# A decoder trunk on one core: the pooling mixer of layer 1 issued in another order, with three advances of the background work per pair of up products

## The chip, the cores and the metric

The kernel runs on one core of a Trainium2 chip. The metric is the device time of one execution, in microseconds, and less is better. The engines named below are TensorE (PE: matrix products), VectorE (DVE), ScalarE (ACT), GpSimd (POOL) and SyncE (SP: it issues the transfers).

## The reference

Sixteen meta tokens are put ahead of 1024 tokens of width 1024; two layers follow. Layer 0 mixes with multi-head latent attention, layer 1 with a causal pooling mixer. After each mixer comes a gated FFN, and RMSNorms stand before and after both.

```python
def pool_mixer(h, w_group, scale):          # windows 2, 4, 8, 16: one per group of 256 channels
    hf = h.reshape(B, L, 4, 256); csum = jnp.cumsum(hf, axis=1)
    means = [(csum_g - csum_g shifted by w) / min(t, w) for each group g, window w]
    mixed = stack(means) - hf
    return einsum('blgc,gcd->blgd', mixed, w_group).reshape(B, L, D) * scale
...
def conv_ffn(h, w_up, conv_w, conv_b, w_down):
    u = h @ w_up                             # 1024 -> 2 * 2816
    u = conv_b + sum(conv_w[j] * up[:, j:j + L] for j in range(3))     # causal
    gate, val = jnp.split(u, 2, axis=-1)
    return (jax.nn.silu(gate) * val) @ w_down
...
for i in range(2):
    m = mla_mixer(a, ...) if i == 0 else pool_mixer(a, ...)            # a = rmsnorm(h)
    h = h + rmsnorm(m);  f = conv_ffn(rmsnorm(h), ...);  h = h + rmsnorm(f)
```

## The kernel before

Channels lie on partitions and tokens along the free axis. The tokens go through in two halves, 536 and 504 of them. Every fp32 product is done as three products of a split into a high and a low part (`ah`, `al` for activations, `wh`, `wl` for weights): ACT casts the high part, DVE subtracts it to give the low part. A weight tile is loaded by SP, cast by ACT (`wh`) and finished by DVE (`wl`); `wh` and `wl` have four buffers each, the pooling weights `pwh` and `pwl` one each.

After attention the program is a row of dense stages: the output projection, then for each layer, each half and each of two parts an `ffn_up` (11 pairs of a gate and a value product, 8 weight blocks of three matmuls each, and each matmul in two cuts for half 0) and an `ffn_down`. An up product ends in PSUM; for half 0 it takes one of three tiles of two banks, for half 1 one of six tiles of one bank. ACT and DVE then apply the convolution (`cv`: one ACT row, two DVE rows), ACT the Silu, DVE the gate (`cv` times `cv`) and the low part `gl`. In layer 0, half 0, DVE first multiplies the product by the late norm factor (`u`).

All norms and the pooling mixer are generators in a list, `self.bg`. `tick()` advances the first of them by one step, that is to its next `yield`, and issues what the step holds with a priority 200 instructions ahead of the place in the code. Before the change `ffn_up` calls `tick()` twice per pair of products, `ffn_down` once per output block, and `drain()` runs what is left at the end of each stage. A scheduler then puts each engine's instructions into one order by these priorities. Each engine runs its own order strictly, so an instruction that waits holds all behind it on that engine.

A norm is `inv_rms_steps`: PE sums squares over channels into `ps_st`, DVE makes the reciprocal root (`nv`, `nyi`, `na`, `nb`, `ny`, `yh`, `yl`) and spreads it over two diagonal tiles (`diag`), PE multiplies these with ones (`ps_bc`), ACT copies the result to `R`. `post` multiplies the mixer's or FFN's output by `R` (`F`), adds it to the residual (`H`) and sums squares (`acc`). `poolmix` takes each of four groups of two channel blocks: `pa` is the normed block, one to four `psm` are window sums, `pmx` the mean less the block (for half 0 two short rows mend the first 16 tokens), and `xh`, `xl` its split. Then come two output blocks of the group's product (`xh`, `xl` with `pwh`, `pwl`). Half 0's mixer is advanced under the `ffn_up` of layer 0, half 1, part 0, and half 1's under that of layer 1, half 0, part 0; the second norm of layer 0's attention runs under that of layer 0, half 0, part 0.

Of the kernel before, what the change touches and what calls it, by code (L numbers as in the profile page):

```python
# [11 lines left out]
F32 = mybir.dt.float32  # L12
F32R = mybir.dt.float32r
I32 = mybir.dt.int32
ALU = mybir.AluOpType
# [6 lines left out]
KD = D // 128  # L22
# [24 lines left out]
class Kern:  # L47
# [561 lines left out]
    def dense(self):  # L609
        tc, nc, io, ctx = self.tc, self.nc, self.io, self.ctx  # L610
        P = lambda name, bufs, **kw: ctx.enter_context(tc.tile_pool(name=name, bufs=bufs, reuse_waits="tile", **kw))
        self.wp, self.ab, self.hp, self.gp = P("wp", 4), P("ab", 1), P("hp", 1), P("gp", 1)
        self.fp, self.up, self.tp = P("fp", 8), P("up", 2), P("tp", 5)
        stp = P("stf", 2, space=PSUM)
        self.stps = lambda name: stp.tile([128, 512], F32, tag="st", name=name)
        self.psum = None
        self.banks(1)
        self.dtile = lambda x: self.tp.tile([128, HALF], F32R, tag="x" + x, name="diag", bufs=2)
        self.H, self.A, self.bg = {}, {}, []

        F, acc = self.wo(0)
        self.bg.append(self.after_mixer(0, F, acc, 0, True))
        F, acc = self.wo(1)
        self.drain()
        self.bg.append(self.after_mixer(1, F, acc, 0, False))
        for L in range(2):
            self.L = L
            for hf in range(2):
                self.banks(2 - hf)
                Fa = None  # L630
                for part in range(2):
                    G = self.ffn_up(hf, part)
                    self.drain()
                    if part == 1 and hf == 0:
                        self.bg.append(self.pre(1, L))
                    if part == 1 and hf == 1 and L == 0:
                        self.bg.append(self.pre(0, 1))
                    if (L, hf, part) == (1, 1, 1):
                        self.ffn_down_last(part, G, Fa)
                        break  # L640
                    F, acc = self.ffn_down(part, G, Fa)
                    Fa = F
                    self.drain()
                else:
                    self.bg.append(self.after_ffn(hf, F, acc, L))
        self.drain()
# [13 lines left out]
    def after_mixer(self, hf, F, acc, L, pre):  # L660
        acc = yield from self.post(hf, F, acc, G_MIXPOST + 8 * L)
        if pre:

            self.late = yield from self.inv_rms_steps(acc, "xh", 2)
            yield from self.pre(hf, L, True)
        else:
            yield from self.ffn_norm(hf, acc)
# [14 lines left out]
    def inv_rms_steps(self, acc, tag, bufs=1, copy=True):  # L682
        yield
        st = self.inv_rms_a(acc, D)
        yield
        yield
        R = self.inv_rms_b(st, self.tp, tag, bufs, HALF, copy)
        yield
        return R[:, :acc.shape[1]]
# [138 lines left out]
    def post(self, hf, F, acc, gcol, last=False, c0=0, tag="Rp"):  # L828


        nc = self.nc
        R = yield from self.inv_rms_steps(acc, tag)
        acc = None
        for k in range(KD):
            nc.vector.scalar_tensor_tensor(F[k], F[k], self.par(gcol + k), R, op0=ALU.mult, op1=ALU.mult)
            h = self.H[hf][k]
            if last:
                s, n = (DEAD if hf == 0 else 0) + c0, F[k].shape[1]
                h = h[:, s:s + n]
            nc.vector.tensor_tensor(h, h, F[k], op=ALU.add)  # L840
            if last:
                s = (HALVES[1][0] - DEAD) * hf + c0
                nc.sync.dma_start(self.io["out"][:, k, s:s + n], h)
            else:
                acc = self.addsq(acc, h)
            if k % 2 == 1:
                yield
        return acc

# [39 lines left out]
    def ffn_up(self, hf, part):  # L889
# [8 lines left out]
        for jj in range(JH):  # L898
            j = part * JH + jj
            cv = []  # L900
            for gv in range(2):
                idx = gv * NJ + j
                u, = self.mm_half(self.wtile(io["w_up"][L, j, :, gv], KD), ah, al, skip=skip)
                if (L, hf) == (0, 0):
                    t = self.up.tile([128, HALF], F32, tag="u", name="u")
                    nc.vector.tensor_tensor(t, u, self.late, op=ALU.mult)
                    u = t
                p0 = G_CONV + (L * 2 * NJ + idx) * 4
                c = self.tp.tile([128, HALF], F32, tag="t", name="cv")[:, :n]
                nc.scalar.activation(c, u[:, pad:pad + n], AF.Identity, bias=self.par(p0 + 3), scale=self.par(p0 + 2))  # L910
                for x in (1, 0):

                    o = max(0, 2 - x - pad)
                    nc.vector.scalar_tensor_tensor(c[:, o:], u[:, pad + x - 2 + o:pad + x - 2 + n], self.par(p0 + x),  # L914
                                                   c[:, o:], op0=ALU.mult, op1=ALU.add)
                cv.append(c)
                if gv == 0:
                    nc.scalar.activation(c, c, AF.Silu)  # L918
                    self.tick()
            nc.vector.tensor_tensor(cv[0], cv[0], cv[1], op=ALU.mult)  # L920
            hi = self.gp.tile([128, HALF], F32R, tag=f"gh{jj}", name="gh")[:, :n]
            lo = self.gp.tile([128, HALF], F32R, tag=f"gl{jj}", name="gl")[:, :n]
            self.split(cv[0], hi, lo, lo_eng="dve")
            gh.append(hi)
            gl.append(lo)
            self.tick()
# [87 lines left out]
    def poolmix(self, hf, R):  # L1014
# [1 line left out]
        F, acc = [], None  # L1016
        n_tok = HALVES[hf][1]
        end = n_tok + 16
        for g in range(4):
            win = 2 << g  # L1020
            xh, xl = [], []
            for kk in range(2):
                k = 2 * g + kk
                a = self.tp.tile([128, HALF + 16], F32, tag="tc", name="pa")[:, :end]
                if hf == 0:
                    nc.gpsimd.memset(a[:, :16], 0.0)
                else:
                    nc.gpsimd.tensor_scalar(a[:, :16], self.phalo[:, k], 1.0, 0.0, op0=ALU.mult, op1=ALU.add)
                nc.vector.scalar_tensor_tensor(a[:, 16:], self.H[hf][k], self.par(G_MIXPRE + 8 + k), R,
                                               op0=ALU.mult, op1=ALU.mult)  # L1030
                if hf == 0:
                    nc.gpsimd.tensor_scalar(self.phalo[:, k], a[:, n_tok:end], 1.0, 0.0,
                                            op0=ALU.mult, op1=ALU.add)
                s = a
                for l in range(g + 1):
                    d = 1 << l
                    lo, hi = 2 * d - 1, end
                    n = self.tp.tile([128, HALF + 16], F32, tag="tc", name="psm")[:, :end]
                    nc.vector.tensor_tensor(n[:, lo:hi], s[:, lo:hi], s[:, lo - d:hi - d], op=ALU.add)
                    s = n  # L1040
                mx = self.tp.tile([128, HALF + 16], F32, tag="tc", name="pmx")[:, :end]
                nc.vector.scalar_tensor_tensor(mx[:, 16:], s[:, 16:], 1.0 / win, a[:, 16:],
                                               op0=ALU.mult, op1=ALU.subtract)
                if hf == 0:
                    nc.vector.tensor_tensor(mx[:, 16:32], s[:, 16:32], self.par(G_CNT + 16 * g, 16), op=ALU.mult)
                    nc.vector.tensor_tensor(mx[:, 16:32], mx[:, 16:32], a[:, 16:32], op=ALU.subtract)
                hi_ = self.tp.tile([128, HALF], F32R, tag="xh", name="xh", bufs=2)[:, :n_tok]
                lo_ = self.tp.tile([128, HALF], F32R, tag="xl", name="xl", bufs=2)[:, :n_tok]
                self.split(mx[:, 16:], hi_, lo_, lo_eng="dve")
                xh.append(hi_)  # L1050
                xl.append(lo_)
                if kk == 0:
                    W = self.wtile(io["w_pool"][g], 4, True)
                yield
            for m in range(2):
                ps = self.mm_half([W[2 * kk + m] for kk in range(2)], xh, xl)
                f = self.fp.tile([128, HALF], F32, tag="F", name="F")[:, :n_tok]
                self.evac(f, ps, self.par(G_PS + 2 * g + m))
                F.append(f)
                acc = self.addsq(acc, f)  # L1060
            yield
        return F, acc


# [50 lines left out]
```

## Time and profile before

| what | value |
|---|---|
| median of 3 runs | 2239.2 us (2238.68 to 2242.64) |
| the profiled execution's own time | 2242.48 us |
| span of its trace | 2240.7 us |
| PE busy in the span | 2151.0 us |
| DVE busy in the span | 1464.8 us |

The span is what the trace covers; 1.8 us of the profiled execution's time lie around it. The trace's times are those of one execution. Shares of busy time are means over stages with different limits.

### The profile page before, as it was taken

How to read it: one execution, taken by the hardware profiler on the slowest of the kernel's cores; microseconds unless marked ns; L12 is line 12 of the kernel's file. 1: busy time of each engine (PE TensorE's matmuls, PEld its weight loads, DVE VectorE, ACT ScalarE, POOL GpSimd, SP SyncE). 2: the span in 40 equal slices, each digit the busy share in tenths (PEclk: the TensorE clock that was granted, in tenths of full speed). 3: DMA queues.
4: the chain of work that ended last, by engine and by line, in shares of the span. 5: the costliest groups of instructions: out<-in, count | busy, mean ns of one | idle time of the engine just before them, and what ended most of it. 6: DMA issues, size and time to landing. Idle time of an engine off the chain costs nothing.

```text
span 2240.7 us, 36251 instructions
## 1 busy us (share of the span) xinstructions
PE 2151.0 (96%) x13890; PEld 1969.4 (88%) x13890; DVE 1464.8 (65%) x2711; ACT 1045.4 (47%) x1932; POOL 385.4 (17%) x732
## 2 busy tenths in 40 slices
PE   8889999998999999999998999999899999999996
PEld 8878888887989999999876888899899998888886
DVE  7877777776489726665877565587745557634656
ACT  6467777776464423433544344344434433433431
POOL 5567676764000000000000000000000000000001
PEclk9999999999999999999999999999999999999998
DMA  5011111114343232233222323422242245223231
GB/s 163 23 35 31 30 34 31 25 55 126 123 161 124 83 105 95 80 97 117 94 71 89 134 96 89 128 83 86 74 142 85 77 128 174 94 84 115 94 94 47
DMA packets 82901, 202.74 MB, mean 90 GB/s; under 512 B 10548, under 2 KB 31668, under 8 KB 82728
## 3 DMA queue, kind: packets, MB, share of 16 engines
q1 hardware_dynamic: 82584, 200.18, 28.4%
q8 instruction: 109, 1.79, 0.3%
q14 instruction: 64, 0.52, 0.1%
q10 hardware_dynamic: 144, 0.25, 0.0%
HBM read 179.15 MB, written 16.97 MB: 88 GB/s over the span
## 4 chain that ended last, share of the span: by engine, by line
PE 86%; DVE 5%; ACT 3%; DMA 2%; POOL 2%; issue 2%; DVEq 0%; SPq 0%; ACTq 0%; POOLq 0%
PE ps_m L766 71%; PE ps_t L587 2%; PE ps_s L536 2%; PE ps_o L572 1%; PE ps_s L538 1%; PE ps_o L573 1%; PE ps_s L537 1%; ACT P L550 1%; DVE ps_s L545 1%; DMA xt<-in_x 1%; PE ps_qk L417 1%; PE ps_qk L418 1%; PE ps_qk L419 1%; PE ps_st L84 1%; DMA or<-heads 0%
## 5 line engine op out<-in xcount | busy, mean ns | idle before, releaser
L70 DVE TENSOR_TENSOR wl<-wr,wh 128x1024 fp32r<-128x1024 f32 (+3 forms) x316 | 348.4, 1103 | 414.2 <-ACT wh L64 403.0
L64 ACT CAST wh<-wr 128x1024 fp32r<-128x1024 f32 (+3 forms) x316 | 301.1, 953 | 587.7 <-PE ps_m L766 513.9
L766 PE MATMUL ps_m<-ah,wh 128*128 128x506 f32 (+2 forms) x2112 | 564.7, 322 | 3.7 <-DVE cv L914 2.0
L766 PE MATMUL ps_m<-al,wh 128*128 128x506 f32 (+2 forms) x2112 | 567.4, 323 | 0.0
L766 PE MATMUL ps_m<-ah,wl 128*128 128x506 f32 (+2 forms) x2112 | 564.1, 321 | 0.0
L766 PEld LDWEIGHTS ps_m<-ah,wh 128*128 128x128 f32 x2112 | 354.2, 190 | 34.7 <-ACT cv L910 2.2
L766 PEld LDWEIGHTS ps_m<-al,wh 128*128 128x128 f32 x2112 | 354.0, 189 | 27.8
L766 PEld LDWEIGHTS ps_m<-ah,wl 128*128 128x128 f32 x2112 | 354.1, 189 | 27.5
L766 PE MATMUL ps_m<-gh,wh 128*128 128x268 f32 (+3 forms) x1088 | 289.1, 318 | 2.2 <-ACT F L775 2.2
L766 PE MATMUL ps_m<-gh,wl 128*128 128x268 f32 (+3 forms) x1088 | 288.0, 317 | 0.0
L766 PE MATMUL ps_m<-gl,wh 128*128 128x268 f32 (+3 forms) x1088 | 287.8, 317 | 0.0
L914 DVE SCALAR_TENSOR_TENSOR cv<-ps_m,params,cv 128x504 f32<-128x504 f32 (+1 forms) x264 | 196.1, 744 | 3.1
L766 PEld LDWEIGHTS ps_m<-gh,wh 128*128 128x128 f32 x1088 | 183.5, 190 | 15.8 <-ACT F L775 2.4
L766 PEld LDWEIGHTS ps_m<-gh,wl 128*128 128x128 f32 x1088 | 182.6, 189 | 13.7
L766 PEld LDWEIGHTS ps_m<-gl,wh 128*128 128x128 f32 x1088 | 182.9, 190 | 13.1
L64 ACT CAST gh<-cv 128x504 fp32r<-128x504 f32 (+2 forms) x88 | 54.7, 622 | 170.3 <-DVE cv L920 170.3
L550 ACT ACTIVATE P<-ps_s,stat 116x812 f32<-116x812 f32 (+9 forms) x160 | 111.4, 698 | 34.6 <-DVE stat L545 26.8
L587 PE MATMUL ps_t<-ident,P 116*116 116x116 f32 x720 | 114.5, 267 | 8.2 <-DVE ptl L601 4.7
L918 ACT ACTIVATE cv<-cv 128x504 f32<-128x504 f32 (+2 forms) x88 | 55.8, 635 | 139.3 <-DVE cv L914 139.3
L555 POOL TENSOR_SCALAR P<-P,stat 116x116 f32<-116x116 f32 (+2 forms) x144 | 108.0, 752 | 52.2 <-DVE stat L553 45.8
L869 POOL TENSOR_SCALAR al<-ahalo 128x2 fp32r<-128x2 f32 x16 | 5.4, 337 | 634.1 <-PE ps_m L766 634.0
L587 PEld LDWEIGHTS ps_t<-ident,P 116*116 116x116 f32 x720 | 83.6, 136 | 22.6 <-DVE ptl L601 5.4
(201 smaller groups left out, 3605.3 us busy)
## 6 DMA issues: line engine op xcount, KB each, us to landing
wr<-in_w_up SPq DMA_DIRECT2D x176, 512.0 KB, 3.5
wr<-in_w_down SPq DMA_DIRECT2D x56, 384.0 KB, 3.1
wr<-in_w_down SPq DMA_DIRECT2D x56, 320.0 KB, 2.9
wr<-in_w_o SPq DMA_DIRECT2D x16, 512.0 KB, 3.7
resid<-H SPq DMA_DIRECT2D x16, 268.0 KB, 4.1
H<-resid SPq DMA_DIRECT2D x16, 268.0 KB, 3.5
xt<-in_x SPq DMA_DIRECT2D x32, 130.0 KB, 2.3
resid<-H SPq DMA_DIRECT2D x16, 252.0 KB, 4.0
```

What stands on the lines that cost most here:

```text
L64: nc.scalar.copy(hi, src)
L70: eng.tensor_tensor(lo, src, hi.bitcast(F32), op=ALU.subtract)
L84: nc.tensor.matmul(ps[:w, i:i + 1], acc[:, w * i:w * i + w], self.ones, start=True, stop=True)
L417: nc.tensor.matmul(ps, wh, xh, start=i == 0, stop=False)
L418: nc.tensor.matmul(ps, wh, xl, start=False, stop=False)
L536: nc.tensor.matmul(ps[:n, x, :w], qh[:, qs], kh[:, ks], start=True, stop=False)
L550: nc.scalar.activation(dst, ps, AF.Exp, bias=mx[:n, 1:2], scale=-1.0, accum_out=es[:n, gi:gi + 1])
L555: nc.gpsimd.tensor_scalar(P[:n, :nk], P[:n, :nk], rs[:n], 1.0, op0=ALU.mult, op1=ALU.mult)
L587: nc.tensor.transpose(pt[:kn, x * QT:x * QT + n], Pi[:n, k0:k0 + kn], self.ident[:n, :n])
L766: nc.tensor.matmul(p, w, x[k][:, skip + c0:skip + c0 + m], start=k == 0 and w is wh and x is xh, stop=k == last and w is wl)
L914: nc.vector.scalar_tensor_tensor(c[:, o:], u[:, pad + x - 2 + o:pad + x - 2 + n], self.par(p0 + x), c[:, o:], op0=ALU.mult, op1=ALU.add)
L918: nc.scalar.activation(c, c, AF.Silu)
```

## The change

`ffn_up` calls its 8 weight blocks as two runs of 4, and on the value product a third `tick()` stands between the two. `post` yields after every fourth block instead of every second; `inv_rms_steps` has one more empty step between its two halves. `poolmix` is cut into `shape(g, kk)` (all that ends in `xh`, `xl`) and `products(g)`. The products of group g-1 are called in the step of the second block of group g, with their priority put 240 instructions back, where they stood behind their own group before, and the whole has nine steps instead of twelve. `xh`, `xl` and `diag` get three buffers instead of two; the pool of `u` is gone, and `u` shares the three buffers of `xl`.

```diff
@@ inv_rms_steps
         st = self.inv_rms_a(acc, D)
+        yield
         yield
         yield
@@ post
-            if k % 2 == 1:
+            if k % 4 == 3:
                 yield
@@ ffn_up
-                u, = self.mm_half(self.wtile(io["w_up"][L, j, :, gv], KD), ah, al, skip=skip)
+                W = self.wtile(io["w_up"][L, j, :, gv], KD)
+                ps = self.mm_half(W[:KD // 2], ah, al, 0, KD, skip=skip, n=n + pad)
+                if gv == 1:
+                    self.tick()
+                u, = self.mm_half(W[KD // 2:], ah, al, KD // 2, KD, ps, skip, n + pad)
                 if (L, hf) == (0, 0):
-                    t = self.up.tile([128, HALF], F32, tag="u", name="u")
+                    t = self.tp.tile([128, HALF], F32, tag="xl", name="u", bufs=3)
@@ poolmix
-        for g in range(4):
...
-            for m in range(2):
-                ps = self.mm_half([W[2 * kk + m] for kk in range(2)], xh, xl)
+        def products(g):
+            nonlocal acc
+            for m in range(2):
+                ps = self.mm_half([W[2 * x + m] for x in range(2)], *X[g])
...
+        for g in range(5):
+            for kk in range(2):
+                if g < 4:
+                    for dst, t in zip(X[g], shape(g, kk)):
+                        dst.append(t)
+                    yield
+                if g and kk == 0:
+                    self.ahead(-240, products, g - 1)
+                if g < 4 and kk == 0:
+                    W = self.wtile(io["w_pool"][g], 4, True)
+        yield
```

Three places show how the order moves. The number after a name counts tiles in the order in which they are made.

PE, layer 0, half 0, part 0, around the second norm of the attention's output, before (`ps_st` sums the squares, `ps_bc` spreads the factor; 72 rows of products stand between the two):

```order
L766 MATMUL ps_m_10230<-ah_9291,wh_10225 128x268 x2
L84 MATMUL ps_st_10056<-ones_66,acc_9697 126x1 x4
L766 MATMUL ps_m_10230<-al_9292,wh_10225 128x268 x2
...
L766 MATMUL ps_m_10420<-ah_9291,wh_10415 128x268 x2
L126 MATMUL ps_bc_10220<-diag_10216,ones_r_68 128x504
L766 MATMUL ps_m_10420<-al_9292,wh_10415 128x268 x2
```

The same place on PE in the changed program:

```order
L767 MATMUL ps_m_10099<-ah_9306,wh_10094 128x268 x2
L767 MATMUL ps_m_10099<-al_9307,wh_10094 128x268 x2
L767 MATMUL ps_m_10099<-ah_9306,wl_10095 128x268 x2
L84 MATMUL ps_st_9797<-ones_66,acc_9632 126x1 x4
L126 MATMUL ps_bc_9961<-diag_9957,ones_r_68 128x504
L126 MATMUL ps_bc_9961<-diag_9959,ones_r_68 128x504
L767 MATMUL ps_m_10161<-ah_9228,wh_10156 128x268 x2
```

And on DVE there (`wl_10351` is the weight tile of the fourth product after `ps_m_10099`, which takes the buffer that this one reads):

```order
L790 TENSOR_TENSOR acc_9632<-acc_9632,sq_9728 128x504
L70 TENSOR_TENSOR wl_10351<-wr_10349,wh_10350 128x1024
L86 TENSOR_SCALAR nv_9802<-ps_st_9797 126x4
L93 TENSOR_SCALAR nyi_9804<-nv_9802 126x4
...
L117 TENSOR_TENSOR diag_9957<-ident_61,yh_9952 126x504
L117 TENSOR_TENSOR diag_9959<-ident_61,yl_9953 126x504
L911 TENSOR_TENSOR u_10020<-ps_m_9971,R_9178 128x536
```

Between `ps_st` and `ps_bc` no product is left on PE, and DVE's order has a `wl` row ahead of `nv`.

PE, layer 0, half 1, part 0, the norm ahead of half 0's pooling in the changed program (`ps_m_14243` is the 11th up product of the part; before, 49 up matmuls stand between this `ps_st` and its `ps_bc`, and the first pooling product nearly two more up products behind that):

```order
L767 MATMUL ps_m_14243<-al_13312,wh_14238 128x506
L84 MATMUL ps_st_13987<-ones_66,acc_13874 67x1 x8
L767 MATMUL ps_m_14243<-ah_13311,wl_14239 128x506
L126 MATMUL ps_bc_14103<-diag_14099,ones_r_68 128x268
L126 MATMUL ps_bc_14107<-diag_14099,ones_r_68 128x268
L126 MATMUL ps_bc_14103<-diag_14101,ones_r_68 128x268
L126 MATMUL ps_bc_14107<-diag_14101,ones_r_68 128x268
L767 MATMUL ps_m_14273<-xh_14157,pwh_14181 128x268
L767 MATMUL ps_m_14274<-xh_14157,pwh_14181 128x268
```

The norm and the first pooling product now stand in one run, with one up matmul between.

PE, the same stage, the pooling products of one group before (up products, 128x506, stand between a group's first `xh` rows and its `xl` rows):

```order
L766 MATMUL ps_m<-ah,wl 128x506
L766 MATMUL ps_m<-xh,pwh 128x268 x4
L766 MATMUL ps_m<-ah,wh 128x506
...
L766 MATMUL ps_m<-ah,wl 128x506
L766 MATMUL ps_m<-xl,pwh 128x268 x2
L766 MATMUL ps_m<-xh,pwl 128x268 x2
L766 MATMUL ps_m<-xl,pwh 128x268 x2
L766 MATMUL ps_m<-xh,pwl 128x268 x2
L766 MATMUL ps_m<-ah,wh 128x506
```

The same in the changed program, from the end of the up product `ps_m_14518` to the start of the next one:

```order
L767 MATMUL ps_m<-ah,wl 128x506
L767 MATMUL ps_m<-xh,pwh 128x268 x4
L767 MATMUL ps_m<-xl,pwh 128x268 x2
L767 MATMUL ps_m<-xh,pwl 128x268 x2
L767 MATMUL ps_m<-xl,pwh 128x268 x2
L767 MATMUL ps_m<-xh,pwl 128x268 x2
L767 MATMUL ps_m<-xh,pwh 128x268 x4
...
L767 MATMUL ps_m<-xh,pwl 128x268 x2
L767 MATMUL ps_m<-xh,pwh 128x268 x4
L767 MATMUL ps_m<-ah,wh 128x506
```

And a piece of DVE's order that goes with it: these rows make the last block of group 1, the blocks of group 2 and the first of group 3 (of 26 rows between the second `cv` row of `ps_m_14518` and the last row of the block `pmx_14504`):

```order
L70 TENSOR_TENSOR xl_14368<-pmx_14363,xh_14367 128x536
L70 TENSOR_TENSOR wl_14803<-wr_14801,wh_14802 128x1024
L1044 TENSOR_TENSOR psm_14444<-psm_14442 128x549
L1044 TENSOR_TENSOR psm_14446<-psm_14444 128x545
L1047 SCALAR_TENSOR_TENSOR pmx_14448<-psm_14446,pa_14438 128x536
L1034 SCALAR_TENSOR_TENSOR pa_14492<-H_13704,params_70,R_14098 128x536
L1050 TENSOR_TENSOR pmx_14448<-psm_14446,params_70 128x16
L1044 TENSOR_TENSOR psm_14496<-pa_14492 128x551
L1051 TENSOR_TENSOR pmx_14448<-pmx_14448,pa_14438 128x16
```

Forty pooling matmuls (the second block of group 1, group 2, and the first four of group 3) stand on PE with no up matmul among them; before, every group's run was parted by up matmuls.

## Rows read from the trace of the kernel before

**Rows 1.** The page's first part: busy us, share of the span, instructions.

```profile
PE 2151.0 (96%) x13890; PEld 1969.4 (88%) x13890; DVE 1464.8 (65%) x2711; ACT 1045.4 (47%) x1932; POOL 385.4 (17%) x732
```

**Rows 2.** Waits of PE, 1102 to 1266 us: total us, times, longest.

```profile
PE ps_m L766 <- DVE psm L1039: 10.1, 1, 10.1
PE ps_m L766 <- ACT xh L64: 4.4, 2, 2.6
```

**Rows 3.** Waits of PE, 1447 to 1670 us.

```profile
PE ps_m L766 <- ACT xh L64: 2.7, 1, 2.7
PE ps_m L766 <- ACT F L775: 2.2, 1, 2.2
```

**Rows 4.** Windows: length, then busy us by engine; granted clock; DMA share, GB/s.

```profile
1102.80:1177.70 74.90, 70.48 (x322) 58.62 (x321) 59.36 (x99) 34.09 (x56) 2.24 (x12) 0.95 0.24 74
1177.70:1265.10 87.40, 77.28 (x375) 64.60 (x375) 56.61 (x108) 32.95 (x56) 0.92 (x3) 0.94 0.36 119
1265.10:1385.00 119.90, 119.90 (x526) 98.83 (x525) 72.64 (x90) 51.28 (x69) 0.00 (x0) 1.00 0.27 88
1584.80:1670.00 85.20, 80.08 (x616) 78.39 (x617) 48.06 (x87) 28.79 (x44) 0.00 (x0) 0.94 0.37 117
1189.80:1194.10 4.30, 4.21 (x13) 3.58 (x14) 3.44 (x8) 0.68 (x2) 0.00 (x0) 0.54 0.02 4
```

**Rows 5.** Timeline of PE: start us, us; in brackets the idle time before.

```profile
1146.65 1.26 PE L766 MATMUL ps_m<-xh,pwh 128*128 128x268 f32 x4 [2.62 <-ACT xh L64]
...
1152.76 0.43 PE L766 MATMUL ps_m<-ah,wh 128*128 128x506 f32 x1
...
1189.89 1.26 PE L766 MATMUL ps_m<-xh,pwh 128*128 128x268 f32 x4 [10.12 <-DVE psm L1039]
1190.95 0.62 PE L766 MATMUL ps_m<-gh,wh 128*128 128x504 f32 x1
...
1193.85 0.39 PE L766 MATMUL ps_m<-gl,wh 128*128 128x504 f32 x1
1194.08 0.39 PE L766 MATMUL ps_m<-gh,wl 128*128 128x504 f32 x1
```

**Rows 6.** Timeline of DVE: a run of `acc`, and a norm's chain.

```profile
643.67 4.53 DVE L789 TENSOR_TENSOR acc<-acc,sq 128x536 f32<-128x536 f32 x7
...
651.23 0.16 DVE L86 TENSOR_SCALAR nv<-ps_st 67x8 f32<-67x8 f32 x1
...
653.69 0.71 DVE L117 TENSOR_TENSOR diag<-ident,yh 67x536 fp32r<-67x536 f32 x1
654.32 0.71 DVE L117 TENSOR_TENSOR diag<-ident,yl 67x536 fp32r<-67x536 f32 x1
```

**Rows 7.** Timeline of PE at the kernel's end.

```profile
2227.21 0.81 PE L126 MATMUL ps_bc<-diag,ones_r 124*128 124x248 f32 x2 [3.20 <-DVE diag L117]
```

**Rows 8.** DVE by form, 1102.8 to 1177.7 us: busy us, mean ns of one.

```profile
L914 DVE SCALAR_TENSOR_TENSOR cv<-ps_m,params,cv 128x504 f32<-128x504 f32 x22 | 16.2, 734 | 0.1
L70 DVE TENSOR_TENSOR wl<-wr,wh 128x1024 fp32r<-128x1024 f32 x8 | 9.7, 1217 | 2.2 <-ACT wh L64 2.2
L1029 DVE SCALAR_TENSOR_TENSOR pa<-H,params,R 128x536 f32<-128x536 f32 x6 | 4.6, 770 | 0.3 <-ACT R L130 0.3
L1039 DVE TENSOR_TENSOR psm<-pa 128x551 f32<-128x551 f32 x6 | 4.4, 735 | 0.2
L1042 DVE SCALAR_TENSOR_TENSOR pmx<-psm,pa 128x536 f32<-128x536 f32 x6 | 4.2, 707 | 0.0
```

**Rows 9.** ACT by form, same stretch.

```profile
L910 ACT ACTIVATE cv<-ps_m,params 128x504 f32<-128x504 f32 x11 | 8.4, 767 | 0.0
L64 ACT CAST wh<-wr 128x1024 fp32r<-128x1024 f32 x8 | 8.4, 1053 | 14.2 <-PE ps_m L766 7.7 <-issue 6.5
L64 ACT CAST xh<-pmx 128x536 fp32r<-128x536 f32 x6 | 3.8, 630 | 0.0
```

**Rows 10.** Timeline of ACT: a norm's copy out of PSUM.

```profile
1112.75 0.67 ACT L130 COPY R<-ps_bc 128x268 f32<-128x268 f32 x2 [0.29 <-PE ps_bc L126]
```

More of the change, by code (lines that the diff above doesn't have):

```diff
@@ L612, in dense @@
         self.wp, self.ab, self.hp, self.gp = P("wp", 4), P("ab", 1), P("hp", 1), P("gp", 1)
-        self.fp, self.up, self.tp = P("fp", 8), P("up", 2), P("tp", 5)
+        self.fp, self.tp = P("fp", 8), P("tp", 5)
         stp = P("stf", 2, space=PSUM)
@@ L617, in dense @@
         self.banks(1)
-        self.dtile = lambda x: self.tp.tile([128, HALF], F32R, tag="x" + x, name="diag", bufs=2)
+        self.dtile = lambda x: self.tp.tile([128, HALF], F32R, tag="x" + x, name="diag", bufs=3)
         self.H, self.A, self.bg = {}, {}, []
@@ L662, in after_mixer @@
         if pre:
-            self.late = yield from self.inv_rms_steps(acc, "xh", 2)
+            self.late = yield from self.inv_rms_steps(acc, "xh", 3)
             yield from self.pre(hf, L, True)
@@ L1018, in poolmix, with shape @@
         end = n_tok + 16
-        for g in range(4):
+        def shape(g, kk):
             win = 2 << g
[L1021 to L1054, printed above, removed]
@@ new lines, in shape @@
+            k = 2 * g + kk
+            a = self.tp.tile([128, HALF + 16], F32, tag="tc", name="pa")[:, :end]
+            if hf == 0:
+                nc.gpsimd.memset(a[:, :16], 0.0)
+            else:
+                nc.gpsimd.tensor_scalar(a[:, :16], self.phalo[:, k], 1.0, 0.0, op0=ALU.mult, op1=ALU.add)
+            nc.vector.scalar_tensor_tensor(a[:, 16:], self.H[hf][k], self.par(G_MIXPRE + 8 + k), R,
+                                           op0=ALU.mult, op1=ALU.mult)
+            if hf == 0:
+                nc.gpsimd.tensor_scalar(self.phalo[:, k], a[:, n_tok:end], 1.0, 0.0,
+                                        op0=ALU.mult, op1=ALU.add)
@@ new lines, in shape @@
+            s = a
+            for l in range(g + 1):
+                d = 1 << l
+                lo, hi = 2 * d - 1, end
+                n = self.tp.tile([128, HALF + 16], F32, tag="tc", name="psm")[:, :end]
+                nc.vector.tensor_tensor(n[:, lo:hi], s[:, lo:hi], s[:, lo - d:hi - d], op=ALU.add)
+                s = n
+            mx = self.tp.tile([128, HALF + 16], F32, tag="tc", name="pmx")[:, :end]
+            nc.vector.scalar_tensor_tensor(mx[:, 16:], s[:, 16:], 1.0 / win, a[:, 16:],
+                                           op0=ALU.mult, op1=ALU.subtract)
@@ new lines, in shape @@
+            if hf == 0:
+                nc.vector.tensor_tensor(mx[:, 16:32], s[:, 16:32], self.par(G_CNT + 16 * g, 16), op=ALU.mult)
+                nc.vector.tensor_tensor(mx[:, 16:32], mx[:, 16:32], a[:, 16:32], op=ALU.subtract)
+            hi_ = self.tp.tile([128, HALF], F32R, tag="xh", name="xh", bufs=3)[:, :n_tok]
+            lo_ = self.tp.tile([128, HALF], F32R, tag="xl", name="xl", bufs=3)[:, :n_tok]
+            self.split(mx[:, 16:], hi_, lo_, lo_eng="dve")
+            return hi_, lo_
@@ L1060, in poolmix @@
                 acc = self.addsq(acc, f)
-            yield
+        X = [([], []) for _ in range(4)]
+        W = None
+        for g in range(5):
[9 more added lines that the diff above has]
+        yield
         return F, acc
```

## The prediction

> **What bounds the kernel now.** I read the page's first part, then the waits of PE, then the windows of the stages that the change touches, and last the timelines of PE and DVE at the single waits. PE is busy for 2151.0 of 2240.7 us [rows 1], so the time is PE's work plus the places where PE stands still or runs at the lower clock; the reader is to look for those places and not for busy engines. Outside the stretch from 1102 to 1670 us the change leaves the dense stages as they are, but for one norm in layer 0, half 0. In a stage with no mixer beside it PE never stops: 119.90 busy of 119.90, DVE busy for 72.64 of that [rows 4], and 526 matmuls in that time are 0.228 us each, or 5.47 for an up product of 24.
>
> Half 0's pooling costs PE 10.1 + 4.4 us of waiting in three waits [rows 2]. Behind two of them the matmuls stay slow for a while: from 1189.89 to 1193.85 us stand four pooling matmuls and seven of 504 columns, which at the 0.23 us between the two rows at 1193.85 and 1194.08, and 0.12 for the shorter ones, need 2.1 us, so 1.9 of the 4.0 are lost [rows 5]. The granted clock there is 0.54 [rows 4], near the lower of the two levels, 1.2 GHz. In the same way the 6.1 us from 1146.65 to 1152.76 (four short matmuls and twelve of 506) lose 2.9 [rows 5]. Sum of half 0: 14.5 + 4.8 = 19.3. Half 1's stretch from 1584.8 has PE busy for 80.08 of 85.20 at a mean clock of 0.94 [rows 4]: 5.1 of idle time, of which [rows 3] name 4.9, and up to as much again in slow matmuls, so about 10. So 29 us is all that a perfect pooling mixer could give back.
>
> **The change part by part.** Work is neither added nor removed: matmuls, DVE rows, casts, loads and stores are the same in number, and cutting an up product into two calls adds no matmul. The third buffers take no time. The transfers of pooling weights and residual blocks move by a few rows in SP's queue; no wait of PE in [rows 2, 3] is put down to a transfer, so I cost that at nothing; the cover is the weight buffers, and if it went, the next up product would be late. What counts is the order: three steps per pair bring the mixer to its end within one part, where a rest used to run in the drain behind it. In half 0, by the order's counts, 59 DVE rows come forward into the time of the last twelve up products. At start-to-start prices (a run of seven `acc` takes 4.53 us, 0.65 each though one lasts 0.71 [rows 6]; `wl` 1.14, `pa` 0.69, `psm`, `pmx` and `cv` 0.65, each its duration less that overlap [rows 8]; small rows of a norm 0.20, from twelve or so between 651.23 and 653.69 [rows 6]) they come to 29.8 us, on top of the 59.4 that DVE already works in 74.9 [rows 4]: 89 us of DVE against about 73 of PE. PE's order sets what that costs.
>
> Term A, the norm in layer 0, half 0. `ps_bc` now stands straight behind `ps_st`. DVE has the `wl` of the fourth product ahead in front of `nv`, and that takes the buffer which `ps_m_10099` has only just released. So behind `ps_st` come a cast of 1.05 [rows 9], a `wl` of 1.14, and the chain from `nv` to the end of the second `diag`, 651.23 to 655.03, 3.8 us [rows 6]: 6.0, with 0.1 for the start of the matmul 6.1. Slow matmuls behind it cost 1.9, the smaller of the two losses above, or 2.9. I take 8.0. The only place where the trace has `ps_bc` behind `ps_st` with nothing between is the kernel's end, where PE waits 3.20 [rows 7]; that is the lower bound (the `wl` already done, no loss of clock), and 9.0 the upper. What was hidden before by some 17 us of products is now bare.
>
> Term B, half 0's mixer. Behind the norm's `ps_st` one up matmul is left. DVE then has eight small rows of the chain (1.6), the two `cv` rows of `ps_m_14243` which wait for its end and for ACT's first row (0.77 + 0.65 + 0.65) and two `diag` (1.3): 5.0 us before `ps_bc` can start. The first pooling product follows directly: the copies to `R` (0.7 [rows 10]), `pa`, `psm`, `pmx`, the next block's `pa` and `psm` and two short rows (3.7 by [rows 8]), and the cast `xh` (0.63 [rows 9]), 5.1 us with PE doing only `ps_bc`. Then one up product and the rest of group 0 run, and group 1's first block beside two up products, with DVE ahead. After `ps_m_14518` come the forty pooling matmuls. Its second `cv` row ends 2.8 us behind it (a `cv` of ACT, two of DVE with a `pmx` between). From there to the block `pmx_14504` DVE has 26 rows, among them two `wl`, nine `psm`, three `acc` and three `xl`, 15.2 us; a cast makes it 18.6 until group 3's first matmul. PE's 36 matmuls ahead of that are 36 x 0.12 = 4.4. PE so waits 14.2 there, in four or five pieces. What is held behind them is the next up product, so also its `cv` and gate. Waits in sum 5.0 + 5.1 + 14.2 = 24.3; slow matmuls behind the two stretches at 2.4 each, the mean of 1.9 and 2.9: 4.8. Against 19.3 before: +9.8. Bounds: if DVE is far enough ahead that the 14.2 vanish, 10.1 + 2.4 - 19.3 = -7; if group 3's second block makes another wait as long as one of the pieces, +14.
>
> Term C, half 1's mixer. Its norms keep their products between `ps_st` and `ps_bc`, and each group's products are parted by up products. DVE's rows in the time of twelve up products come to 84.1 by the same prices, PE's to 80.2: 3.9 of waiting at least, with two slow stretches 8.7, against 10 before: -1.5, between -10 (all hidden) and +4.
>
> Sum 8.0 + 9.8 - 1.5 = +16.3. On the profiled execution that is 2242.5 + 16.3 = 2258.8; this execution is 3.3 over the median of the runs, 2239.2, so I forecast 2255. With all lower bounds 3.2 - 7 - 10 = -14, with all upper ones +27.
>
> **The rivals.** First, a gain. The products of a group now stand a step behind the shape of its last block, so `xh` and `xl` could be done when PE comes to them. The three waits of [rows 2] were all of that kind, and PE has six tiles to run on, so DVE may lag by several products of 5.47 us before an up product is held; an excess of 16 us of DVE would fit into that and be worked off under `ffn_down`, where DVE has 28 us less to do than before. Half 0's 19.3 would vanish and term A stay at its bare chain: 2239.2 - 19.3 + 3.2 = 2223. The Trainium skill speaks for this: its page "Perfetto Trace Analysis", section "Optimization Strategy", says that where the most-contended engine changes over time, interleaving such stretches may help. Here the mixer's stretch was already interleaved and DVE busy for 59.36 of 74.90 there [rows 4]. Against this rival stands the run of forty matmuls: PE is in order, so no tile helps while a pooling matmul waits at the head. It decides if DVE reaches `pmx_14504` within 4 us of the end of `ps_m_14518` instead of 18.
>
> Second, no change: the stalls only move. If DVE's excess of 16 us is the whole loss of half 0 in place of 19.3, term A is the bare 3.2 and half 1 stays, the sum is -0.1: 2239.
>
> Third, heavier: term A at 9, term B at +14 and half 1 at +4, as each norm and each group waits with a loss of clock behind it: 2266. For it speaks that two of three waits in [rows 5] and [rows 2] had such a loss; against it, that half 1's products are spread.
>
> **How the numbers follow.** The forecast, 2244 to 2262, has a chance of 0.54; the heavier case, 2262 and more, 0.10; no change, within 0.2% or 4.5 us (about what a measurement of this kernel can tell from nothing), 0.18; the gain 0.18. The range of 8 in 10 runs from 2229, which leaves out the better half of the gain, to 2267, above the sum of all upper bounds. Slower 0.64, same 0.18, faster 0.18. The likeliest case's own range is 2244 to 2262.
>
> **What the profile after would show.** Term A: a wait of PE at `ps_bc` for `diag` of 5 to 6.5 us under layer 0, half 0's `ffn_up`; 3 would say that the `wl` came early. Term B: a second such wait of about 5 ahead of half 0's pooling, a wait of about 5 for the first `xh`, and four or five waits for `xh`, `xl` of 2 to 4.5 between two up products, with a granted clock near 0.5 behind each stretch; a window of DVE there near full, and the drain behind with far less of DVE than before. Term C: small waits, none over 4. The prediction is wrong if the waits for `xh` and `xl` are gone (the gain), or if PE's wait for `diag` is absent in both places; a wait for a `cv` or `u` by an up product would be a cause that I did not count.

## The result, and the profile after

The changed kernel takes 2262.76 us (median of 4 runs, 2260.96 to 2264.61), the kernel before in the same sessions 2240.27. The ratio is 1.0097, with a 95% interval of 1.0085 to 1.011: slower by 22.5 us, on the side that was forecast and inside the range of 8 in 10 runs (2229 to 2267), but 0.8 us above the likeliest case's own range of 2244 to 2262, and 6 us more than the sum gave. The profiled execution has a span of 2260.7 us, 20.0 more than that of the kernel before, whose profiled execution lay 2.2 us above its median.

The page's first part, to be read beside [rows 1]:

```profile
PE 2156.9 (95%) x13890; PEld 1973.3 (87%) x13890; DVE 1465.0 (65%) x2711; ACT 1046.6 (46%) x1932; POOL 390.0 (17%) x732
```

The counts are the same, and DVE's busy time too (1465.0 to 1464.8): nothing was added. PE's busy time is 6 us longer with the same matmuls, since more of them ran at the lower clock; the rest of the 20 us of span is idle time. The waits of PE, from three stretches (layer 0, half 0; layer 0, half 1; layer 1, half 0), beside [rows 2, 3]:

```profile
PE ps_bc L126 <- DVE diag L117: 4.1, 1, 4.1
...
PE ps_m L767 <- ACT xh L64: 15.5, 4, 5.3
PE ps_bc L126 <- DVE diag L117: 4.4, 1, 4.4
PE ps_m L767 <- DVE xl L70: 1.8, 1, 1.8
...
PE ps_m L767 <- ACT xh L64: 4.8, 3, 2.9
PE ps_m L767 <- DVE xl L70: 2.6, 2, 1.4
PE ps_m L767 <- DVE cv L919: 2.6, 2, 1.4
PE ps_m L767 <- ACT F L778: 1.3, 2, 0.8
```

The first stretch had no wait at all before. In the second, 14.5 us of waits have become 21.7: two of them are the bare norm (4.4 for `diag`) and the longest `xh` (5.3) right behind it. In the third, 11.3 us stand where the two rows of [rows 3] name 4.9, and all waits of that stretch before 7.9. These rows of the kernel before belong to it: the window of the first stretch (columns as in [rows 4]), and the waits of the third that [rows 3] leave out.

```profile
643.00:741.00 98.00, 97.98 (x798) 97.81 (x799) 85.98 (x159) 44.63 (x61) 0.00 (x0) 1.00 0.38 126
...
PE ps_m L766 <- DVE cv L914: 2.0, 1, 2.0
PE ps_m L766 <- DVE xl L70: 0.7, 1, 0.7
PE ps_m L766 <- ACT F L777: 0.3, 1, 0.3
```

The windows of the changed kernel show what DVE did and what clock was granted:

```profile
714.50:720.90 6.40, 6.26 (x24) 5.55 (x25) 6.40 (x11) 3.41 (x5) 0.00 (x0) 0.50 0.23 71
...
1095.00:1143.00 48.00, 38.38 (x188) 32.26 (x186) 36.94 (x69) 18.56 (x29) 2.20 (x9) 0.86 0.13 41
1118.60:1123.60 5.00, 4.91 (x14) 4.11 (x15) 4.62 (x11) 0.91 (x3) 0.72 (x2) 0.50 0.00 0
1143.00:1163.00 20.00, 7.92 (x33) 6.76 (x32) 19.39 (x33) 10.61 (x20) 6.78 (x6) 0.61 0.34 114
1163.00:1178.00 15.00, 15.00 (x67) 12.71 (x66) 8.40 (x14) 5.29 (x10) 0.38 (x1) 0.83 0.17 56
...
1540.00:1570.00 30.00, 24.45 (x148) 22.37 (x147) 27.42 (x42) 13.84 (x22) 1.81 (x3) 0.83 0.28 92
```

From 1143 to 1163 us PE works for 7.92 of 20.00 us while DVE works for 19.39: the run of forty. PE's timeline names the pieces, with the bare norm of layer 0, half 0 ahead of it:

```profile
709.46 1.04 PE L84 MATMUL ps_st<-ones,acc 128*126 128x1 f32 x8
714.64 1.38 PE L126 MATMUL ps_bc<-diag,ones_r 126*128 126x504 f32 x2 [4.14 <-DVE diag L117]
...
1148.32 1.26 PE L767 MATMUL ps_m<-xh,pwh 128*128 128x268 f32 x4 [4.66 <-ACT xh L64]
1151.39 0.82 PE L767 MATMUL ps_m<-xl,pwh 128*128 128x268 f32 x2 [1.82 <-DVE xl L70]
1156.99 1.26 PE L767 MATMUL ps_m<-xh,pwh 128*128 128x268 f32 x4 [3.44 <-ACT xh L64]
1162.20 1.26 PE L767 MATMUL ps_m<-xh,pwh 128*128 128x268 f32 x4 [2.17 <-ACT xh L64]
```

These are the four pieces that the prediction spoke of, 12.1 us in sum. DVE at the bare norm:

```profile
710.32 1.23 DVE L70 TENSOR_TENSOR wl<-wr,wh 128x1024 fp32r<-128x1024 f32 x1 [0.91 <-ACT wh L64]
711.46 0.15 DVE L86 TENSOR_SCALAR nv<-ps_st 126x4 f32<-126x4 f32 x1
...
713.91 0.68 DVE L117 TENSOR_TENSOR diag<-ident,yh 126x504 fp32r<-126x504 f32 x1
714.50 0.68 DVE L117 TENSOR_TENSOR diag<-ident,yl 126x504 fp32r<-126x504 f32 x1
```

`ps_st` ends at 710.5, the `wl` ahead of `nv` at 711.5, and the chain at 715.2. Only 1 us of the `wl` is on the path, since the cast ran beside `ps_st`. The first `ps_bc` starts at 714.64, when the first of the two `diag` is done (714.59), and the second at 715.2, when the other is.

### The profile page after: what moved, and what is told of

Same layout as the page of the kernel before. It is cut to its first block, busy times and chain, and to the rows that moved or that the text cites. A ratio compares the mean times of both kernels' runs of the same rounds, so it can differ in the third digit from the quotient of the medians.

```text
span 2260.7 us, 36223 instructions
## 1 busy us (share of the span) xinstructions
PE 2156.9 (95%) x13890; PEld 1973.3 (87%) x13890; DVE 1465.0 (65%) x2711; ACT 1046.6 (46%) x1932; POOL 390.0 (17%) x732
## 4 chain that ended last, share of the span: by engine, by line
PE 83%; DVE 7%; ACT 3%; DMA 2%; issue 2%; POOL 2%; SPq 0%; DVEq 0%; ACTq 0%; POOLq 0%
PE ps_m L767 70%; PE ps_t L587 2%; PE ps_s L536 2%; PE ps_o L572 1%; PE ps_o L573 1%; PE ps_s L538 1%; PE ps_s L537 1%; ACT P L550 1%; DMA xt<-in_x 1%; DVE ps_s L545 1%; PE ps_qk L417 1%; PE ps_qk L418 1%; PE ps_qk L419 1%; DMA or<-heads 0%; PE ps_bc L126 0%
## 5 line engine op out<-in xcount | busy, mean ns | idle before, releaser
L70 DVE TENSOR_TENSOR wl<-wr,wh 128x1024 fp32r<-128x1024 f32 (+3 forms) x316 | 348.4, 1102 | 435.3 <-ACT wh L64 431.9
L915 ACT ACTIVATE cv<-ps_m,params 128x504 f32<-128x504 f32 (+1 forms) x132 | 101.5, 769 | 9.9 <-PE ps_m L767 9.9
```

The costliest lines, as they stand in the source:

```text
L70: eng.tensor_tensor(lo, src, hi.bitcast(F32), op=ALU.subtract)
```

## The experiments

Three theories stood against each other. **Theory 1**: the third advance per pair draws the halves of a norm together and brings the pooling products into long runs that wait for DVE. **Theory 2**: putting the products a step back makes the waits. **Theory 3**: the shared buffers of `u` and `xl` do. The kernel before took 2240.3 to 2241.5 in the sessions, as a median of 4 to 17 runs.

### The third advance taken out

```diff
-                if gv == 1:
-                    self.tick()
```

> The changed kernel with the third advance per pair taken out, all else kept. Theory 1 (the third advance draws the norms' two halves together and packs the pooling products into one run of forty): the order now has 7 and 11 us of products between the sums and the spread in the two norms, and no run over 24 matmuls, so the time is 2232 to 2244. Theory 2 (putting the products a step back makes the waits): no less than 2255. Theory 3 (the shared buffers of u and xl): 2263.

Measured: 2223.54 us (2223.24 to 2225.78), ratio to before 0.992 [0.9906, 0.9933]. It beats both kernels, by 17.9 us the one before and by 39.2 the changed one, which is more than theory 1 expected. Theories 2 and 3 fall as causes by themselves: all that they name is still there. Its waits of PE in the two mixer stretches:

```profile
PE ps_m L767 <- ACT xh L64: 5.5, 2, 3.2
PE ps_m L767 <- DVE xl L70: 0.9, 1, 0.9
...
PE ps_m L767 <- DVE cv L917: 4.1, 2, 2.1
PE ps_m L767 <- ACT F L778: 0.3, 1, 0.3
```

No `diag` is left there, and 6.4 us of product waits stand where there were 14.5 before.

### Three more empty steps in each norm

```diff
         yield
         yield
         yield
+        yield
+        yield
+        yield
         R = self.inv_rms_b(st, self.tp, tag, bufs, HALF, copy)
```

> The changed kernel with three more empty steps between the two halves of each norm. Both bare norms get products between their halves again (7 and 11 us by the order), the run of forty stays. Theory 1: the norm of layer 0, half 0 gives back its 7.6 us and the one ahead of half 0's pooling about 5, the forty keep their waits of some 18: 2247 to 2253. Theories 2 and 3: no change, 2263.

Measured: 2239.62 us (2237.58 to 2242.60), ratio 0.9992 [0.9984, 1.0001]. It gives back 23.1 us, about ten more than theory 1 expected, and against theories 2 and 3. I had not counted that the 5.3 us wait for the first `xh` is part of the bare norm (it is gone here; the three `xh` waits of the run of forty are still there, 4.7 the longest). So the two norms and what hangs on them cost most of 23 us, and the run of forty stays.

### The pooling mixer of before, with three advances

```diff
-            self.ahead(-240, products, g - 1)
+            for m in range(2):
+                ps = self.mm_half([W[2 * kk + m] for kk in range(2)], xh, xl)
```

> The changed kernel with the pooling mixer of before (products right behind their group's shapes, twelve steps), the third advance kept. Both norms stay bare in the order, and each group's products stand in a run of twenty with four ahead. Theory 1: the bare norms keep 7.6 and about 7 us and the four runs wait for their own group's rows, 2255 to 2270. Theory 2: 2240 to 2248, since the products are no longer put back. Theory 3: 2263.

Measured: 2272.33 us (2270.34 to 2274.92), ratio 1.0136 [1.0122, 1.015]. Slower by another 9.6: against theories 2 and 3, and 2 us over theory 1's range.

### The pooling mixer of the change alone

The kernel before with `poolmix` replaced, two buffers for `xh` and `xl`, and nothing else:

```diff
-            for m in range(2):
-                ps = self.mm_half([W[2 * kk + m] for kk in range(2)], xh, xl)
...
+                if g and kk == 0:
+                    self.ahead(-240, products, g - 1)
```

> The kernel before with the pooling mixer of the change alone (nine steps, products a step back), two advances per pair, all buffers and norms of before. Theory 1: no wait is added and the products' waits shrink, 2230 to 2242. Theory 2: 2250 or more. Theory 3: 2240.

Measured: 2227.72 us (2224.38 to 2230.22), ratio 0.9935 [0.9923, 0.9948]. It is 2 us below theory 1's range, and against theories 2 and 3: the mixer of the change is a gain of 14 us by itself. What in it gains is not shown by this run, since the products stand a step back and the mixer has nine steps instead of twelve. In the kernel before, the longest wait, the 10.1 us of [rows 2], stands behind the last up matmul of the part and ahead of the first of `ffn_down`, where the rest of the mixer is drained (24 pooling matmuls stand in one run there, so not every group was parted by up matmuls before); here all pooling products are through before the first of `ffn_down`, and that wait is gone. Nine steps alone may do that. The 4.2 us from here to the run with two advances lie in the buffers, `post`'s longer steps, the added step in the norm and the two calls per up product together; which of them it is was not tried.

### The third advance alone

The kernel before with the two runs of four blocks and the tick between, and nothing else:

```diff
+                ps = self.mm_half(W[:KD // 2], ah, al, 0, KD, skip=skip, n=n + pad)
+                if gv == 1:
+                    self.tick()
+                u, = self.mm_half(W[KD // 2:], ah, al, KD // 2, KD, ps, skip, n + pad)
```

> The kernel before with the third advance per pair alone (the value product in two runs of four blocks, an advance between); pooling mixer, norms and buffers of before. In the order the norm ahead of half 0's pooling is bare, the norm in layer 0, half 0 keeps its products, each pooling group is a run of twenty with four ahead. Theory 1: the time of the run with the old mixer, 2272, less its 7.2 us for the norm in layer 0: 2260 to 2268. Theory 2 (putting back is needed for a loss): 2241.

Measured: 2271.56 us (2269.79 to 2273.20), ratio 1.0135 [1.0122, 1.0148]. So +30.7 us on the kernel before, some 4 over the expected range; on the changed kernel it is +39.2. Most of the difference is the norm of layer 0, half 0, which is not bare here (6.1 us, by the runs with the third advance in one stage). The wait for `diag` ahead of the mixer is 6.9 here, and each of half 0's four groups waits for its own `xh`; the last three rows are DVE's wait in the stretch of the last three of these, the window of that stretch, and the window of the 7.45 us wait in it:

```profile
PE ps_m L766 <- ACT xh L64: 31.6, 7, 7.5
PE ps_bc L126 <- DVE diag L117: 6.9, 1, 6.9
...
DVE acc L789 <- ACT sq L788: 11.8, 2, 6.0
...
1126.50:1186.00 59.50, 39.56 (x174) 33.20 (x174) 42.73 (x72) 22.09 (x36) 1.87 (x9) 0.86 0.17 60
...
1146.90:1154.90 8.00, 0.55 (x3) 0.13 (x1) 8.00 (x15) 3.38 (x5) 0.32 (x2) 0.82 0.29 108
```

DVE is busy all through the wait, but only for 42.73 of the 59.50 us: in these it waits 11.8 us for the squares of the pooling products (`acc` for `sq`). With each group's products right behind its shapes, PE and DVE wait for each other in turn; a DVE that is full is not the whole cause here.

### The products not put back by 240

```diff
-                    self.ahead(-240, products, g - 1)
+                    self.ahead(0, products, g - 1)
```

> The changed kernel with the products' priority put back by nothing instead of 240, still a step behind their group. The order keeps both bare norms and a run of forty. Theory 1: within 4 us of the changed kernel, 2259 to 2267, since the run of forty comes from three advances per pair. Theory 2: 2240 to 2250.

Measured: 2264.84 us (2260.54 to 2267.55), ratio 1.0104 [1.009, 1.0117]: as the changed kernel, by theory 1.

### The products put back by 480, three more empty steps

```diff
-                    self.ahead(-240, products, g - 1)
+                    self.ahead(-480, products, g - 1)
```

> The changed kernel with three more empty steps in each norm and the products put back by 480 instead of 240. In the order a run of 28 and one of 44 now stand 11 us of up products later. Theory 1a (the run waits because it stands ahead of DVE's rows): the 18 us of waits and slow matmuls of the run shrink to under 4, and half 1's 13 to under 5, 2212 to 2225. Theory 1b (DVE has 16 us more work than PE in that stretch, wherever the products stand): the waits go over to the up products for their cv rows, 2232 to 2240.

Measured: 2238.36 us (2235.85 to 2241.60), ratio 0.9989 [0.9981, 0.9998]. That is the time of the run with three empty steps alone (2239.62). The traces show why: against that run, the 480 did not move the head of the run. In both, 432 up matmuls of the part stand ahead of it (336 in the changed kernel), and the long waits fall at the same times, first in the run with the three empty steps alone, then in this one:

```profile
1149.61 1.26 PE L770 MATMUL ps_m<-xh,pwh 128*128 128x268 f32 x4 [4.75 <-ACT xh L64]
1158.53 1.26 PE L770 MATMUL ps_m<-xh,pwh 128*128 128x268 f32 x4 [4.18 <-ACT xh L64]
```

```profile
1149.40 1.26 PE L770 MATMUL ps_m<-xh,pwh 128*128 128x268 f32 x4 [3.61 <-ACT xh L64]
1158.36 1.26 PE L770 MATMUL ps_m<-xh,pwh 128*128 128x268 f32 x4 [4.54 <-ACT xh L64]
```

The waits for `xh`, `xl` and `pwh` come to 12.4 us there and 11.8 here. So theory 1a was not put to the test: that products further behind DVE's rows would wait less is neither shown nor ruled out. By time it is 1b, but not by its place: the waits stay at `xh` and do not go over to the `cv`. The windows of this run:

```profile
1095.00:1145.00 50.00, 49.53 (x249) 41.75 (x248) 44.14 (x80) 23.40 (x37) 2.28 (x9) 1.00 0.20 65
1145.00:1163.00 18.00, 7.25 (x31) 6.09 (x29) 17.23 (x30) 9.54 (x19) 1.14 (x5) 0.62 0.30 100
```

DVE is busy for 44.1 of 50.0 us ahead of the run and for 17.2 of 18.0 in it, so it has little room to catch up.

### The products put back by 480, two advances

The third advance taken out as in the first experiment, and 480 as in the one above.

> Two advances per pair with the mixer of the change and its products put back by 480. Theory 1: the 10.3 us that the run with two advances and 240 still loses at three product waits from 1163 to 1178 shrink to under 3: 2213 to 2219. If DVE is the limit there: 2222 to 2225.

Measured: 2226.06 us (2222.95 to 2232.14), ratio 0.9934 [0.992, 0.9948]: no gain over 240, and 1 us above the range for DVE as the limit. One `xh` wait of 5.5 us is left. Its product stands behind 504 up matmuls of the part, as the same product does with 240, so this run does not decide between the two either.

### The third advance in one stage alone

Three kernels, each with two advances elsewhere; the pair in brackets is (0, 0), (0, 1) and (1, 0).

```diff
-                if gv == 1:
+                if gv == 1 and (L, hf) == (0, 0):
```

> The changed kernel with the third advance kept only in layer 0, half 0, two advances elsewhere. In the order only the norm there is bare. Theory 1: the run with two advances everywhere, 2223.5, plus the 7.6 us that the trace of the changed kernel loses there: 2229 to 2233. If the loss of that norm is hidden once the rest is spread: 2223.

> The third advance kept only in layer 0, half 1, where half 0's mixer runs: bare norm ahead of the mixer and the run of forty. Theory 1: the trace loses 31.7 us in that stage with three advances and 10.3 with two, so 2223.5 + 21.4 = 2245, from 2241 to 2249.

> The third advance kept only in layer 1, half 0, where half 1's mixer runs. Theory 1: 17.1 us of loss there with three advances, 6.2 with two, so 2223.5 + 10.9 = 2234, from 2230 to 2238. The forecast had this stage at no loss, which would be 2222 to 2225.

Measured: 2229.68 us (2227.70 to 2232.68), 2244.93 (2243.04 to 2250.51) and 2232.95 (2231.68 to 2236.85), with ratios to before of 0.9949 [0.9936, 0.9961], 1.002 [1.0012, 1.0029] and 0.9965 [0.9951, 0.9978]. Over the 2223.54 of two advances that is 6.1, 21.4 and 9.4 us, all in their ranges; the sum, 36.9, is 94% of the 39.2 that the third advance costs in all three places. The one wait for `diag` in the first of them is that of the changed kernel:

```profile
PE ps_bc L126 <- DVE diag L117: 4.2, 1, 4.2
```

### Two advances, products not put back by 240

The third advance taken out, and 0 in place of 240.

> Two advances per pair, mixer of the change, products a step behind their group but with their priority put back by nothing. If the step behind is what helps: 2220 to 2227. If the 240 instructions are needed on top: 2230 to 2240, as the products then wait for their rows as in the kernel before.

Measured: 2226.72 us (2225.42 to 2227.56), ratio 0.9934 [0.9921, 0.9946]. It is in the range for the step behind; the 240 add some 3 us. That it is the step behind, and not the nine steps, stays argued: both are kept here.

## Why the prediction was right, and where it was off

**The direction and its cause** held: the order brings work of DVE forward into a stretch where DVE has little room, and PE, in order, waits at the norm and at the run of forty. The forecast sum was +16.3, measured +22.5. A tally over the traces (for each matmul, how much later than is usual for its form the next one starts) gives for the three stages, each with the `ffn_down` behind it, 1.9, 20.3 and 14.7 us before and 9.4, 31.9 and 17.5 after: +7.5, +11.6 and +2.8, for the terms +8.0, +9.8 and -1.5. The sum, 21.9, is more than the 20.0 us of span, since what lies ahead of these stages took 1.9 less in this execution.

**Term A** (8.0) was right in place and near in size: 6.1 by the run that has the third advance only there. Its two parts were off in opposite ways, so its size is in part luck. The wait was 4.1 and not 6.1, because the cast of the `wl` ran beside `ps_st` and the first `ps_bc` did not wait for the second `diag`; the slow matmuls cost about 3.1, not 1.9 (24 matmuls in 6.26 us at a granted clock of 0.50).

**Term B** (29.1 of loss after, +9.8) held piece by piece: 4.4 for 5.0, 5.3 for 5.1, 12.1 in four waits for 14.2. What was too small is the clock. I had 4.8 for two slow stretches; but inside the run of forty PE also works at a mean clock of 0.61 over 20 us, so its few matmuls there take longer as well, and the stretch from 1163 on has 0.83 over 15 us. The tally of the stage, 31.9, is 2.8 over the 29.1.

**Term C** (-1.5) has the wrong sign, and this is the step that failed: "each group's products are parted by up products", from which I took DVE's excess of 3.9 us as the whole wait. The waits in this stage are 11.3 us, 3.4 more than before, and 17.5 us are lost in all where the term had 8.7. Part of that was cancelled by a second slip: the 10 of before counted only from 1584.8 on, and the tally of the whole stage gives 14.7. Of the 11.3, 2.6 are for `cv` and 1.3 for `F`, which the term did not count. The run with the third advance only there costs 9.4 over two advances. DVE worked for 27.42 of 30.00 us from 1540 to 1570, with PE's waits there again at `xh` and `xl`: a few up products between the groups did not help where DVE had so little room.

**The gain rival** was right that waits can be taken away, and wrong about its balance: with two advances the mixer of the change gains 14 us. The time that I worked out for this rival, 2223, is that of the run with two advances, but by luck: it let half 0's 19.3 us vanish and kept 3.2 for the norm, whereas that run keeps about 10 of half 0's, loses nothing more at the norm, and gains about 8 in half 1's stage. I weighed the change as one thing. With the two parts priced apart, the mixer is worth -14, and the third advance +31 on the kernel before and +39 on the changed one. What the Trainium skill says in "Perfetto Trace Analysis", section "Optimization Strategy", that interleaving stretches with different busiest engines may help, agrees with the run with two advances, where no pooling product waits behind the part's last up matmul any more; the changed kernel shows its limit, with DVE busy for 19.39 of 20.00 us.

**No change** did not come. **Heavier** was to begin at 2262, and 2262.8 lies just inside it. Its ground came in part: half 1's stage rose by about 3 where it had +4, against the forecast's own reason that half 1's products are spread. What stays open, besides the share of the nine steps in the 14 us, is what would take away the 6.4 us of waits that half 0's mixer keeps with two advances. DVE is again near full there, in the windows of that run:

```profile
1100.00:1163.00 63.00, 63.00 (x306) 53.28 (x305) 56.99 (x98) 31.89 (x50) 4.10 (x13) 1.00 0.25 82
1163.00:1173.00 10.00, 3.59 (x16) 2.64 (x15) 9.23 (x17) 6.67 (x13) 0.89 (x2) 0.72 0.24 72
```

DVE makes the low parts of weights for later products among these rows (two `wl` of 1.14 in the run of forty of the changed kernel); whether it is these that make `xh` late was not tried.

## What to carry to other kernels

Background work that is advanced by a count of steps has a pace, and the pace has to fit the engine that the work needs, not the one that it hides behind: here two advances per pair leave 6.4 us of product waits in half 0's mixer (2223.5 us), and three leave 21.7 with the norm (2262.8). A chain that goes PE, DVE, PE (a norm) needs products on PE between its two ends that last as long as the DVE part, about 4 us here; whoever shortens the steps around it should look at the order for the two ends standing together. A change of several parts is to be priced part by part, since a gain of one (14 us) can lie under the loss of another.

## What the runs showed of the hardware

The same wait does not always bring the lower clock. In the run with two advances PE waits 2.09 us for a `cv` in half 1's stage, and its matmuls go on at full pace; in the run with two advances and 480 the same wait, 2.10 us, is followed by slow ones:

```profile
1570.61 0.48 PE L767 MATMUL ps_m<-ah,wh 128*128 128x260 f32 x2 [2.09 <-DVE cv L917]
1570.93 0.41 PE L767 MATMUL ps_m<-al,wh 128*128 128x260 f32 x2
```

```profile
1571.25 0.77 PE L767 MATMUL ps_m<-ah,wh 128*128 128x260 f32 x2 [2.10 <-DVE cv L917]
1571.82 0.64 PE L767 MATMUL ps_m<-al,wh 128*128 128x260 f32 x2
```

The granted clock over the 4.5 us behind it is 1.00 in the first and 0.62 in the second. So a wait of about 2 us cost either nothing or some 1.5 us more. The waits of 4.1, 5.3 and 10.1 us looked at here all had a slow stretch behind them, of 4 to 6 us at a granted clock of 0.50, 0.50 and 0.54, and its length did not grow with the wait.
